# Strassen's gate and up products on normalised inputs, with one Silu operation and six steps' first products at the front

## The chip, the cores and the metric

The kernel runs on 1 core of one Trainium2 chip. The metric is device time in microseconds, the median of several executions. Besides them one execution is recorded by the hardware profiler. Engines are named as in the profile: PE (TensorE: matmuls), DVE (VectorE), ACT (ScalarE), POOL (GpSimd) and SP (which issues DMAs). Each engine works through its own instructions in order.

## The reference, cut to what matters

One layer of an encoder on 2048 new frames and 32 sample frames, width 1024. All matrices are float32. The change touches only the feed-forward part of the last frames:

```python
x = x + jnp.concatenate([att, pool], axis=-1) @ w_out
h2 = _rmsnorm(x, g_ffn)          # x * rsqrt(mean(x*x) + 1e-6) * g_ffn, per frame
x = x + (jax.nn.silu(h2 @ w_ffn_gate) * (h2 @ w_ffn_up)) @ w_ffn_down
gate = jax.nn.sigmoid(_rmsnorm(x, g_ple) @ w_ple_gate)
x = x + (p @ w_ple) * gate
```

`w_ffn_gate` and `w_ffn_up` are 1024 x 2816, `w_ffn_down` 2816 x 1024.

## The kernel before, in words

Activations lie with channels on partitions and frames in columns. Float32 accuracy comes from three matmuls per term (`mm3`, lines 214 to 216): each operand is split into a rounded high half and a low half, and high x high, high x low and low x high are summed in PSUM. A split (lines 179 and 180, for whole weight columns 198 and 199) is a cast on ACT and a subtraction on DVE.

The stage `rest` takes output blocks in three pairs; the last pair (b0 and b1, 352 frames each) is the `tail`. There the order is: output projection `w_out` with the residual, eight products per block (each 24 matmuls), then the feed-forward part, then the gated embedding. PE's order is the written order; the order of the other engines is a scheduler's.

In the tail the gate and up products use Strassen's scheme (Winograd's form): two halves of the 1024 input channels by two neighbouring output columns f and f+1 by two blocks b0 and b1, with seven products of quarter size (12 matmuls each) instead of eight. There are 22 steps, gate and up in turn. The products of a step, with weight x input, are: a11 x (b0, first half), a12 x (b0, second half), s1 x t1, s2 x t2, then s4 x (b1, second half), s3 x t3, a22 x t4. s1 to s4 are sums of the quarter weights, made by POOL (`sums`, line 960). t1 to t4 are sums over blocks and halves of the inputs (`combine`, made beside the projection of b1). The first product's result is copied out of PSUM by ACT as p1, the third (p5) stays in its bank until after the sixth, and the results are DVE additions (lines 1197, 1220, 1224, 1228).

The inputs before are x times the gain, without the per-frame factor of the norm (`rbc`, 1 / rms in every row). It is put in behind the products: `evac` multiplies a gate result by rbc (line 1179, DVE), takes Sigmoid (1181, ACT), multiplies by the result (1182, POOL) and by rbc once more (1187, POOL) for the up product; an up result is multiplied by that (1190, DVE) and split. `norm1` and `norm2` make rbc: column sums on PE, a power on POOL, a spread over partitions on PE, a copy by ACT. Down products of a group of output columns (`down`) stand behind the first step of the next group, those of the last group behind the last step.

Weights go through three buffers each of raw, high and low tiles (`RAW_BUFS, W_BUFS`); in the tail two units are prepared ahead of the one in use. PSUM banks of products rotate: `mm_bank` counts up, and in the tail six banks follow each other, so a product takes the bank of the product six before it:

```python
if phase["tail"] and phase["mm"] % 6 > 3:
    p, tag = ((ps_z, "z"), (ps_av, "av"))[phase["mm"] % 2]
    return p.tile([128, 512], F32, tag=tag, name=nm("mm"))
if phase["tail"] and phase["mm"] % 6 == 3 or ...
    return ps_x.tile([128, 512], F32, tag="x", name=nm("mm"))
return ps_mm.tile([128, 512], F32, tag="mm", name=nm("mm"))   # three banks
```

Of the kernel before, what the change touches and what calls it, by code (L numbers as in the profile page):

```python
# [78 lines left out]
def stickbreak_step(  # L79
# [794 lines left out]
    def rest(sup, pool, apool):  # L874
# [66 lines left out]
        def load_quad(wsrc, f):  # L941
# [5 lines left out]
            r = {"a11": a1[:, :4], "a12": a1[:, 4:]}  # L947
# [14 lines left out]
        QUADS = ("a11", "a12", "s1", "s2", "s4", "s3", "a22")  # L962
# [3 lines left out]
        def plan_quads():  # L966
            run = []

            def emit(items):
                hi = wpool.tile([128, 2, 4, 128], F32R, tag="whi", name=nm("whi"), bufs=W_BUFS)  # L970
                lo = wpool.tile([128, 2, 4, 128], F32R, tag="wlo", name=nm("wlo"), bufs=W_BUFS)
                for i, (j, key) in enumerate(items):
                    for n in (j, j + 1):
                        if n < len(steps) and n not in raws and (n == j or key == "s4"):
                            raws[n] = load_quad(*steps[n])
                    if key not in raws[j]:
                        sums(raws[j])
                    split(raws[j][key], hi[:, i], lo[:, i])
                return hi, lo, len(items)

            def close():
                for i in range(0, len(run), 2):
                    wplan.append(lambda items=run[i:i + 2]: emit(items))
                run.clear()

            for i, fs in enumerate(groups):
                FIRST[len(steps)] = i
                for f in fs[::2]:
                    steps.append((w_gate, f))
                    steps.append((w_up, f))  # L990
            for j in range(len(steps)):
                run.extend((j, key) for key in QUADS)
                i = FIRST.get(j)
                if i:
                    close()
                    plan_down(groups[i - 1])
            close()
            plan_down(groups[-1])

        quad = {"at": 0, "n": 0}  # L1000

        def next_quad():

            if quad["at"] == quad["n"]:
                quad["w"] = wunit()
                quad["at"], quad["n"] = 0, quad["w"][2]
            i = quad["at"]
            quad["at"] += 1
            return quad["w"][0][:, i], quad["w"][1][:, i]
# [23 lines left out]
        def combine(oc):  # L1033

            b0, b1 = sup
            k = oc % 4
            if oc < 4:
                H["d"] = tmp(b1, "t1")
                V.tensor_sub(H["d"], X[b1][oc], X[b0][oc])
                S.activation(H["d"], H["d"], AF.Copy, scale=gcol("ffn", oc))  # L1040
                keep_h("t1", k, H["d"])
                square(b1, oc)
                return
            def less(x, y):
                t = tmp(b1, "sg")
                V.scalar_tensor_tensor(out=t, in0=x, scalar=gcol("ffn", oc), in1=y, op0=ALU.mult, op1=ALU.subtract)
                return t
            ready_h(b1, oc, "ffn")
            t2 = less(X[b1][oc], H["d"])
            keep_h("t2", k, t2)  # L1050
            h12 = tmp(b1, "t2")
            S.activation(h12, X[b1][k], AF.Copy, scale=gcol("ffn", k))
            t3 = less(X[b1][oc], h12)
            t4 = tmp(b1, "t2")
            V.scalar_tensor_tensor(out=t4, in0=X[b0][oc], scalar=gcol("ffn", oc), in1=t2, op0=ALU.mult, op1=ALU.subtract)
            keep_h("t3", k, t3)
            keep_h("t4", k, t4)
# [4 lines left out]

        OC = {b: range(KC) for b in sup}
        if sup == OS[-1]:
            OC[sup[1]] = [c + 4 * e for c in range(4) for e in range(2)]
        for b in sup:
            for oc in OC[b]:
# [24 lines left out]
        for b in sup:  # L1092
            if b == 0:
                yield BUBBLE
            for i, oc in enumerate(OC[b]):
# [5 lines left out]
                if tail and b == sup[1]:  # L1101
                    combine(oc)
                    if i == 1:
                        norm1(sup[0])
                    if i == 3:
                        norm2(sup[0])
# [58 lines left out]
        def strassen():  # L1165
# [8 lines left out]
            def evac(j, x, b, t):  # L1174
# [3 lines left out]
                if src is w_gate:  # L1178
                    V.tensor_mul(t, t, rbc[b])  # L1179
                    sg = tmp(b, "sg")  # L1180
                    S.activation(sg, t, AF.Sigmoid)
                    GP.tensor_mul(sg, sg, t)
                    if x == 0 and b == b0:
                        g = ap.tile([128, 385], F32, tag="keep", name=nm("g"), bufs=5)[:, :n]
                    else:
                        g = pool.tile([128, OMAX], F32, tag="xs", name=nm("g"), bufs=X_SLOTS)[:, :n]
                    GP.tensor_mul(g, sg, rbc[b])
                    sgr[f, b] = g
# [10 lines left out]

            for j in range(len(steps)):  # L1200
                pa = mm_bank()[:, :n]
                yield from prod(pa, [h[b0][k] for k in range(4)])
                p1 = ap.tile([128, WMAX], F32, tag="bot", name=nm("p1"), bufs=3)[:, :n]
                S.copy(p1, pa)
# [259 lines left out]
```

## Time and profile before

| | |
|---|---|
| median of 3 runs | 2895.23 us (2890.81 to 2901.4) |
| profiled execution, its own time | 2899.64 us |
| its span, first to last instruction | 2897.9 us, mean granted clock 0.988 |
| PE, DVE, ACT, POOL busy | 97%, 76%, 47%, 28% |
| output projection of b1 ends, first step starts | about 2281 us |
| last step of the scheme ends | about 2761 us |

Times in the trace are microseconds from the span's start. A row of the timeline gives start, duration, engine, line, operation, tiles written and read, shape, and in square brackets the idle time before it and what ended it. PEclk is the granted clock of PE as a share of 2.4 GHz: 0.50 is the level of 1.2 GHz.

### The profile page before, as it was taken

The page shows a single profiled execution, that of the slowest core. Times are in us where ns is not written, and L with a number is a line of the kernel's source. Part 1 is how long each engine was busy: PE and PEld are TensorE (multiplying, and loading weights), DVE is VectorE, ACT ScalarE, POOL GpSimd, SP SyncE. Part 2 cuts the span into 40 slices and gives each one's busy share as a digit, 9 for nine tenths or more (in the row PEclk, how much of TensorE's full clock was granted, in tenths as well). Part 3 has the DMA queues.
Part 4 walks back from the last instruction along what each step waited for, and adds up shares of the span by engine and source line. Part 5 has one row for each costly group of instructions (what it writes and reads, how often), then busy time and mean ns, then how long its engine had stood idle before and what let it go on. Part 6 is the DMA issues. An engine that isn't in the chain of part 4 may idle for free. (4 is left out here: it accounts for less than half of the span.)

```text
span 2897.9 us, 50355 instructions
## 1 busy us (share of the span) xinstructions
PE 2796.9 (97%) x18214; PEld 2747.3 (95%) x18214; DVE 2202.5 (76%) x3738; ACT 1362.8 (47%) x2986; POOL 817.3 (28%) x1311
## 2 busy tenths in 40 slices
PE   8999999899999999989999999999999899999998
PEld 7998989899999999989999999999999899999998
DVE  6476798797877777887888777777555887787676
ACT  5455666464444444455554444444343532333343
POOL 2021233132222213232332211212132653554320
PEclk9999999899999999999999999999999999999999
DMA  6867747773333333323753243333236322221233
GB/s 206 240 191 209 217 147 226 227 221 94 106 103 100 94 93 94 110 86 110 223 143 97 88 123 103 96 103 98 86 88 202 114 70 73 73 74 58 63 90 119
DMA packets 522274, 366.51 MB, mean 126 GB/s; under 512 B 63005, under 2 KB 509277, under 8 KB 522026
## 3 DMA queue, kind: packets, MB, share of 16 engines
q1 hardware_dynamic: 483914, 350.51, 40.4%
q10 hardware_dynamic: 38112, 12.79, 1.7%
q8 instruction: 144, 2.36, 0.3%
q14 instruction: 104, 0.85, 0.1%
HBM read 292.89 MB, written 70.32 MB: 125 GB/s over the span
## 5 line engine op out<-in xcount | busy, mean ns | idle before, releaser
L214 PE MATMUL mm<-as,whi 128*128 128x352 f32 (+1 forms) x3628 | 1207.0, 333 | 27.4 <-DVE t L1197 19.6
L215 PE MATMUL mm<-as,whi 128*128 128x352 f32 (+1 forms) x3628 | 1170.4, 323 | 0.0
L216 PE MATMUL mm<-as,wlo 128*128 128x352 f32 (+1 forms) x3628 | 1165.8, 321 | 1.7 <-DVE wlo L180 1.1
L214 PEld LDWEIGHTS mm<-as,whi 128*128 128x128 f32 x3628 | 687.5, 190 | 34.0 <-issue 21.4
L216 PEld LDWEIGHTS mm<-as,wlo 128*128 128x128 f32 x3628 | 687.1, 189 | 2.5 <-DVE wlo L180 1.5
L215 PEld LDWEIGHTS mm<-as,whi 128*128 128x128 f32 x3628 | 686.9, 189 | 0.6 <-DVE as L913 0.3
L198 ACT CAST whi<-wraw 128x1024 fp32r<-128x1024 f32 x282 | 295.9, 1050 | 264.8 <-PE mm L215 248.5
L742 DVE TENSOR_TENSOR_SCAN keep<-keep,keep,zeros 128x384 f32<-128x384 f32 (+2 forms) x328 | 317.3, 967 | 112.4 <-ACT keep L727 111.6
L199 DVE TENSOR_TENSOR wlo<-wraw,whi 128x1024 fp32r<-128x1024 f32 x279 | 347.9, 1247 | 59.0 <-ACT whi L198 57.4
L727 ACT ACTIVATE keep<-z 128x384 f32<-128x384 f32 (+3 forms) x464 | 195.4, 421 | 361.7 <-PE z L724 305.7
L739 POOL COPY keep<-keep 128x1 f32<-128x1 f32 (+1 forms) x328 | 147.8, 451 | 442.2 <-DVE keep L742 441.7
L743 DVE TENSOR_TENSOR beta<-beta,keep 128x384 f32<-128x384 f32 (+3 forms) x464 | 237.8, 513 | 32.5 <-POOL beta L732 1.4
L180 DVE TENSOR_TENSOR aa<-tp,aa 128x384 fp32r<-128x384 f32 (+4 forms) x472 | 213.5, 452 | 14.4 <-ACT aa L179 13.2
L724 PE MATMUL z<-kt,q 128*128 128x384 f32 (+4 forms) x928 | 212.1, 310 | 12.5 <-ACT beta L728 12.3
L179 ACT CAST aa<-tp 128x384 fp32r<-128x384 f32 (+4 forms) x472 | 192.9, 409 | 62.3 <-PE tp L753 52.3
L1161 DVE TENSOR_TENSOR xs<-xs,mm 128x352 f32<-128x352 f32 (+1 forms) x288 | 143.6, 510 | 81.3 <-PE mm L216 80.0
L753 PE MATMUL tp<-ident,beta 128*128 128x128 f32 (+1 forms) x1112 | 199.7, 274 | 2.2 <-DVE xt L342 1.5
L214 PE MATMUL mm<-hh,whi 128*128 128x384 f32 (+2 forms) x576 | 198.9, 345 | 2.3 <-ACT yt L457 1.0
L906 POOL TENSOR_TENSOR acc<-acc,sq 128x352 f32<-128x352 f32 (+1 forms) x112 | 119.7, 1068 | 285.3 <-ACT sq L905 277.1
L728 ACT ACTIVATE beta<-z 128x384 f32<-128x384 f32 (+3 forms) x464 | 194.4, 419 | 7.2 <-ACT keep L727 5.2
L1140 POOL TENSOR_TENSOR sg<-sg,t 128x336 f32<-128x336 f32 (+1 forms) x88 | 103.1, 1171 | 324.5 <-ACT sg L1115 313.6
L215 PE MATMUL mm<-hl,whi 128*128 128x384 f32 (+2 forms) x576 | 186.5, 324 | 1.2 <-DVE hl L336 1.2
(202 smaller groups left out, 4660.2 us busy)
## 6 DMA issues: line engine op xcount, KB each, us to landing
wraw<-in_w_ffn_down_dram SPq DMA_DIRECT2D x66, 512.0 KB, 3.5
wraw<-in_w_ffn_gate_dram SPq DMA_DIRECT2D x55, 512.0 KB, 3.9
wraw<-in_w_ffn_up_dram SPq DMA_DIRECT2D x55, 512.0 KB, 4.0
wraw<-in_w_in_dram SPq DMA_DIRECT2D x48, 512.0 KB, 4.9
wraw<-in_w_out_dram SPq DMA_DIRECT2D x48, 512.0 KB, 5.3
kt<-ks SPq DMA_DIRECT2D x112, 192.0 KB, 2.5
vt<-vs SPq DMA_DIRECT2D x112, 192.0 KB, 2.8
wraw<-in_w_ple_gate_dram SPq DMA_DIRECT2D x32, 512.0 KB, 4.0
```

Of the source, the lines that this page charges most:

```text
L180: V.tensor_sub(lo, src, hi.bitcast(F32))
L198: S.copy(hi, raw)
L199: eng.tensor_sub(lo, raw, hi.bitcast(F32))
L214: T.matmul(ps, a[0], b[0], start=first, stop=False)
L215: T.matmul(ps, a[0], b[1], start=False, stop=False)
L216: T.matmul(ps, a[1], b[0], start=False, stop=last)
L724: T.matmul(z[:qw, :wi], hd["q"][:, e, qsl], un["k"][:, :wi], start=(e == 0), stop=(e == 1))
L727: S.activation(keep[:qw, :wi], z[:qw, :wi], AF.Sigmoid, scale=-0.125)
L728: S.activation(beta[:qw, :wi], z[:qw, :wi], AF.Sigmoid, scale=0.125)
L742: V.tensor_tensor_scan(rev, rev, zeros[:qw].broadcast_to([qw, wi]), initial=init, op0=ALU.mult, op1=ALU.add)
L743: V.tensor_mul(beta[:qw, :wi], beta[:qw, :wi], keep[:qw, 1:wi + 1])
L753: T.transpose(bank[:kw, qo[i]:qo[i] + qws[i]], un["b"][i][:qws[i], k0:k0 + kw], ident[:qws[i], :qws[i]])
```

## The change

The inputs of the scheme are normalised (gain and rbc in one DVE operation, `normed`), so a gate result needs one ACT operation, Silu, and an up result is multiplied by it. b0's inputs are made beside b1's projection (`first_inputs`); b1's and t1 to t4 need b1's norm and are made after it (`other_inputs`). Two products of a step, those that read b0 alone, become a helper `front`; those of the first six steps (`AHEAD`) run ahead of everything else, and b1's norm and `other_inputs` are written behind the first and second of them. Units of weights no longer run over steps: a11 with a12 (one split of a whole column), s1 with s2, s4 with s3, a22 alone. The first column of the first six steps is loaded once more for the front.

```diff
-        QUADS = ("a11", "a12", "s1", "s2", "s4", "s3", "a22")
+        UNITS = (("a11", "a12"), ("s1", "s2"), ("s4", "s3"), ("a22",))
+        AHEAD = 6
...
+            for j in range(AHEAD):
+                plan_col(steps[j][0], steps[j][1] * 128)
             for j in range(len(steps)):
-                run.extend((j, key) for key in QUADS)
...
+                for keys in UNITS[j < AHEAD:]:
+                    wplan.append(lambda j=j, keys=keys: emit(j, keys))
...
-        def combine(oc):
...
+        def normed(t, b, c):
+            V.scalar_tensor_tensor(out=t, in0=X[b][c], scalar=gcol("ffn", c), in1=rbc[b], op0=ALU.mult, op1=ALU.mult)
+            return t
+        def first_inputs(c):
...
+            H["n", c] = normed(H["pair"][:, c % 2, :N[sup[0]]], sup[0], c)
+            keep_h("h11" if c < 4 else "h21", c % 4, H["n", c])
+        def other_inputs():
...
+            for k in range(4):
+                h12[k] = normed(tmp(b1, ("acc", "sg")[k // 2]), b1, k)
+                t1 = tmp(b1, "t1")
+                V.tensor_sub(t1, h12[k], H["n", k])
+                keep_h("t1", k, t1)
+            for k in range(4):
+                h22 = normed(extra(), b1, 4 + k)
+                t3 = tmp(b1, "t2")
+                V.tensor_sub(t3, h22, h12[k])
+                t2 = extra()
+                V.tensor_add(t2, t3, H["n", k])
+                keep_h("t2", k, t2)
+                keep_h("h22", k, h22)
+                keep_h("t3", k, t3)
+                t4 = tmp(b1, "t1")
+                GP.tensor_sub(t4, H["n", 4 + k], t2)
+                keep_h("t4", k, t4)
...
                 if src is w_gate:
-                    V.tensor_mul(t, t, rbc[b])
-                    sg = tmp(b, "sg")
-                    S.activation(sg, t, AF.Sigmoid)
-                    GP.tensor_mul(sg, sg, t)
...
-                    GP.tensor_mul(g, sg, rbc[b])
...
+                    S.activation(g, t, AF.Silu)
...
+            def front(j):
+                pa = mm_bank()[:, :n]
+                yield from prod(pa, [H["h11", k] for k in range(4)])
...
+                S.copy(p1[j], pa)
+                pa = mm_bank()[:, :n]
+                yield from prod(pa, [H["h21", k] for k in range(4)])
+                evac(j, 0, b0, plus("t1", pa, p1[j]))
+            for j in range(AHEAD):
+                yield from front(j)
+                if j == 0:
+                    norm1(b1)
+                if j == 1:
+                    norm2(b1)
+                    other_inputs()
             for j in range(len(steps)):
...
+                if j >= AHEAD:
+                    yield from front(j)
```

DVE at the front. Before, the end of the last combination (t2, t3, t4 of the eighth channel block) stands right ahead of the first step's first addition (L1197):

```order
L913 SCALAR_TENSOR_TENSOR as_6030_28915<-xs_6028_28887,gt_95,as_6030_28915 128x352
L1046 SCALAR_TENSOR_TENSOR sg_6032_28921<-xs_6028_28887,gt_95,t1_6018_28863 128x352
L1046 SCALAR_TENSOR_TENSOR sg_6035_28928<-xs_6028_28887,gt_95,t2_6034_28926 128x352
L1055 SCALAR_TENSOR_TENSOR t2_6036_28930<-xs_5927_28453,gt_95,sg_6032_28921 128x352
L180 TENSOR_TENSOR as_6033_28923<-sg_6032_28921,as_6033_28923 128x352
L180 TENSOR_TENSOR t3_6008_28816<-sg_6035_28928,t3_6008_28816 128x352
L180 TENSOR_TENSOR t4_6038_28935<-t2_6036_28930,t4_6037_28934 128x352
L180 TENSOR_TENSOR wlo_6041_28940<-s3_6026_28879,whi_6040_28939 128x512
L1197 TENSOR_TENSOR t1_6047_28978<-mm_6046_28965,p1_6045_28963 128x352
```

Now the end of `other_inputs` stands ahead of the third front pair's addition (L1198, t1_6069, which reads mm_6068), and the fourth pair's stands four rows on:

```order
L1031 SCALAR_TENSOR_TENSOR hx_6055_29014<-xs_5988_28794,gt_95,rbc_6010_28913 128x352
L180 TENSOR_TENSOR as_6049_28999<-hx_6048_28997,as_6049_28999 128x352
L180 TENSOR_TENSOR as_6050_29002<-hx_6046_28993,as_6050_29002 128x352
L180 TENSOR_TENSOR t4_6054_29011<-t1_6052_29008,t4_6053_29010 128x352
L1057 TENSOR_TENSOR t2_6056_29016<-hx_6055_29014,sg_6024_28943 128x352
L1059 TENSOR_TENSOR hx_6057_29018<-t2_6056_29016,hn_5958_28650 128x352
L180 TENSOR_TENSOR t3_6051_29005<-t2_6056_29016,t3_6051_29005 128x352
L1198 TENSOR_TENSOR t1_6069_29068<-mm_6068_29055,p1_6067_29053 128x352
L180 TENSOR_TENSOR as_6058_29020<-hx_6057_29018,as_6058_29020 128x352
L180 TENSOR_TENSOR as_6059_29023<-hx_6055_29014,as_6059_29023 128x352
L180 TENSOR_TENSOR t4_6062_29031<-t1_6060_29028,t4_6061_29030 128x352
L1198 TENSOR_TENSOR t1_6077_29106<-mm_6076_29093,p1_6075_29091 128x352
```

What moved: all additions of the front from the third pair on are queued behind the 42 rows of `other_inputs` and the weight splits among them.

DVE in a gate step (step 8). Before, an rbc multiply (L1179) follows each of the four results:

```order
L1197 TENSOR_TENSOR t1_6360_30658<-mm_6357_30639,p1_6356_30637 128x352
L1179 TENSOR_TENSOR t1_6360_30658<-t1_6360_30658,rbc_5985_28715 128x352
L180 TENSOR_TENSOR wlo_6366_30681<-wraw_6351_30599,whi_6365_30680 128x512 x2
L1197 TENSOR_TENSOR t2_6367_30698<-mm_6364_30679,p1_6356_30637 128x352
L1197 TENSOR_TENSOR acc_6368_30700<-mm_6363_30666,t2_6367_30698 128x352
L1220 TENSOR_TENSOR acc_6368_30700<-mm_6369_30702,acc_6368_30700 128x352
L180 TENSOR_TENSOR wlo_6374_30724<-s1_6375_30725,whi_6373_30723 128x512
L1179 TENSOR_TENSOR acc_6368_30700<-acc_6368_30700,rbc_6059_29032 128x352
L180 TENSOR_TENSOR wlo_6374_30724<-s2_6376_30727,whi_6373_30723 128x512
L1224 TENSOR_TENSOR t2_6367_30698<-mm_6372_30722,t2_6367_30698 128x352
L1197 TENSOR_TENSOR t1_6379_30750<-mm_6363_30666,t2_6367_30698 128x352
L1179 TENSOR_TENSOR t1_6379_30750<-t1_6379_30750,rbc_6059_29032 128x352
```

Now the step holds additions and weight splits alone:

```order
L1198 TENSOR_TENSOR t1_6364_30608<-mm_6363_30595,p1_6362_30593 128x352
L180 TENSOR_TENSOR wlo_6368_30614<-a22_6328_30419,whi_6367_30613 128x512
L1198 TENSOR_TENSOR t2_6370_30642<-mm_6369_30629,p1_6362_30593 128x352
L1198 TENSOR_TENSOR acc_6371_30644<-mm_6366_30612,t2_6370_30642 128x352
L180 TENSOR_TENSOR wlo_6374_30648<-wraw_6357_30569,whi_6373_30647 128x1024
L1236 TENSOR_TENSOR acc_6371_30644<-mm_6372_30646,acc_6371_30644 128x352
L1240 TENSOR_TENSOR t2_6370_30642<-mm_6376_30666,t2_6370_30642 128x352
L180 TENSOR_TENSOR wlo_6381_30686<-s1_6382_30687,whi_6380_30685 128x512
L1198 TENSOR_TENSOR t1_6377_30680<-mm_6366_30612,t2_6370_30642 128x352
L180 TENSOR_TENSOR wlo_6381_30686<-s2_6383_30689,whi_6380_30685 128x512
L1244 TENSOR_TENSOR t2_6370_30642<-mm_6379_30684,t2_6370_30642 128x352
```

What moved: four rows are gone, and the whole first column of the next step is split in one row.

POOL after b1's norm (r_6001), now: the sums of steps 0 and 1 (L960) and the four subtractions that make t4 (L1064, into t1 tiles):

```order
L268 TENSOR_TENSOR r_6001_28871<-ss_5999_28863,mhalf_93 128x3
L252 MEMSET ss_7149_34742 128x3
L960 TENSOR_TENSOR s2_6086_29123<-s1_6085_29121,wraw_6080_29113 128x512
L960 TENSOR_TENSOR s3_6087_29125<-wraw_6080_29113,a21_6081_29115 128x512
L960 TENSOR_TENSOR s4_6088_29127<-wraw_6080_29113,s2_6086_29123 128x512
L960 TENSOR_TENSOR s1_6112_29247<-a21_6095_29167,a22_6096_29169 128x512
L1064 TENSOR_TENSOR t1_6034_28966<-hn_5967_28696,hx_6030_28955 128x352
L960 TENSOR_TENSOR s3_6114_29251<-wraw_6094_29165,a21_6095_29167 128x512
L960 TENSOR_TENSOR s2_6113_29249<-s1_6112_29247,wraw_6094_29165 128x512
L1064 TENSOR_TENSOR t1_6043_28987<-hn_5967_28696,hx_6039_28976 128x352
L960 TENSOR_TENSOR s4_6115_29253<-wraw_6094_29165,s2_6113_29249 128x512
L1064 TENSOR_TENSOR t1_6052_29008<-hn_5976_28742,hx_6048_28997 128x352
```

What moved: the t4 subtractions, DVE's before, stand in POOL's queue among the weight sums.

## Rows read from the trace of the kernel before

**Rows 1.** The page: busy time, share and instructions of each engine.

```profile
PE 2796.9 (97%) x18214; PEld 2747.3 (95%) x18214; DVE 2202.5 (76%) x3738; ACT 1362.8 (47%) x2986; POOL 817.3 (28%) x1311
```

**Rows 2.** PE's waits, 2180 to 2898 us: total, times, longest.

```profile
PE mm L214 <- DVE t L1197: 19.6, 10, 5.4
PE mm L214 <- ACT as L179: 4.5, 1, 4.5
```

**Rows 3.** Busy time by stretches: length, PE, PEld, DVE, ACT, POOL, PEclk, DMA.

```profile
2275.00:2330.00 55.00, 46.32 (x264) 44.73 (x263) 47.80 (x72) 24.35 (x49) 33.93 (x27) 0.91 0.26 76
2330.00:2690.00 360.00, 340.15 (x2070) 336.51 (x2069) 282.24 (x410) 116.33 (x212) 176.70 (x133) 0.98 0.24 72
2690.00:2770.00 80.00, 74.79 (x451) 73.70 (x450) 56.09 (x86) 23.82 (x43) 23.54 (x19) 0.96 0.20 60
2510.00:2570.00 60.00, 60.00 (x376) 59.82 (x375) 42.59 (x64) 17.64 (x34) 26.79 (x20) 1.00 0.23 67
...
2582.00:2586.00 4.00, 4.00 (x14) 4.00 (x15) 3.88 (x6) 2.27 (x5) 2.07 (x2) 0.50 0.00 0
```

**Rows 4.** DVE's timeline from a gate step's end into the up step.

```profile
2386.02 1.26 DVE L1179 TENSOR_TENSOR t<-t,rbc 128x352 f32<-128x352 f32 x1
2387.21 1.77 DVE L180 TENSOR_TENSOR wlo<-s,whi 128x512 fp32r<-128x512 f32 x1
...
2399.99 0.52 DVE L1197 TENSOR_TENSOR t<-mm,t 128x352 f32<-128x352 f32 x1
```

**Rows 5.** PE's timeline, the two places named.

```profile
2400.66 0.41 PE L214 MATMUL mm<-as,whi 128*128 128x352 f32 x1 [3.45 <-DVE t L1197]
...
2766.06 0.66 PE L214 MATMUL mm<-as,whi 128*128 128x352 f32 x1 [4.53 <-ACT as L179]
```

**Rows 6.** DVE's timeline while POOL stands still.

```profile
2281.38 0.57 DVE L1055 SCALAR_TENSOR_TENSOR t<-xs,gt,sg 128x352 f32<-128x352 f32 x1
2281.88 0.52 DVE L180 TENSOR_TENSOR as<-sg,as 128x352 fp32r<-128x352 f32 x1
2282.31 0.52 DVE L180 TENSOR_TENSOR t<-sg,t 128x352 fp32r<-128x352 f32 x1
...
2283.18 0.68 DVE L180 TENSOR_TENSOR wlo<-wraw,whi 128x512 fp32r<-128x512 f32 x1
...
2284.82 0.52 DVE L1039 TENSOR_TENSOR t<-xs,xs 128x352 f32<-128x352 f32 x1
```

**Rows 7.** DVE's timeline while POOL works without a break.

```profile
2269.68 2.31 DVE L199 TENSOR_TENSOR wlo<-wraw,whi 128x1024 fp32r<-128x1024 f32 x1
2271.92 0.51 DVE L1100 TENSOR_TENSOR xs<-xs,mm 128x352 f32<-128x352 f32 x1
...
2274.15 1.60 DVE L1039 TENSOR_TENSOR t<-xs,xs 128x352 f32<-128x352 f32 x1
```

**Rows 8.** POOL's timeline in the same stretch.

```profile
2269.44 1.48 POOL L960 TENSOR_TENSOR s<-s,wraw 128x512 f32<-128x512 f32 x1 [1.37 <-DMA wraw<-in_w_ffn_gate_dram]
2270.88 2.27 POOL L960 TENSOR_TENSOR s<-wraw,a 128x512 f32<-128x512 f32 x1
2273.10 2.27 POOL L960 TENSOR_TENSOR s<-wraw,s 128x512 f32<-128x512 f32 x1
```

**Rows 9.** Groups by line and form, 2240 to 2766 us: count, busy, mean.

```profile
L180 DVE TENSOR_TENSOR wlo<-s,whi 128x512 fp32r<-128x512 f32 x88 | 80.9, 929 | 0.7 <-ACT whi L179 0.2
L1187 POOL TENSOR_TENSOR g<-sg,rbc 128x352 f32<-128x352 f32 x44 | 55.1, 1255 | 2.1
L1179 DVE TENSOR_TENSOR t<-t,rbc 128x352 f32<-128x352 f32 x33 | 31.0, 940 | 0.8
```

**Rows 10.** DVE's timeline ahead of the last product group.

```profile
2761.39 1.23 DVE L199 TENSOR_TENSOR wlo<-wraw,whi 128x1024 fp32r<-128x1024 f32 x1
2762.53 0.52 DVE L1190 TENSOR_TENSOR t<-t,g 128x352 f32<-128x352 f32 x1
```

**Rows 11.** Groups by line: the activation table load.

```profile
L727 ACT ACT_TABLE_LOAD x1 | 1.3, 1283 | 0.0
```

More of the change, by code (lines that the diff above doesn't have):

```diff
@@ L946, in load_quad @@
             dma(a1, w[:, :, :128])
[L947 removed]
+            r = {"a1": a1, "a11": a1[:, :4], "a12": a1[:, 4:]}
             for key, k in (("a21", 0), ("a22", 4)):
@@ L966, in plan_quads, with emit @@
         def plan_quads():
[L967 to L976, printed above, removed]
-                        sums(raws[j])
[L978 to L984, printed above, removed]
+            def emit(j, keys):
+                for n in (j, j + 1):
+                    if n < len(steps) and n not in raws and (n == j or keys[0] == "s4"):
+                        raws[n] = load_quad(*steps[n])
+                hi = wpool.tile([128, KC, 128], F32R, tag="whi", name=nm("whi"), bufs=W_BUFS)
+                lo = wpool.tile([128, KC, 128], F32R, tag="wlo", name=nm("wlo"), bufs=W_BUFS)
+                if keys[0] == "a11":
+                    split(raws[j]["a1"], hi, lo)
+                else:
+                    if keys[0] == "s1":
+                        sums(raws[j])
+                    for i, key in enumerate(keys):
+                        split(raws[j][key], hi[:, 4 * i:4 * i + 4], lo[:, 4 * i:4 * i + 4])
+                return hi, lo, len(keys)
             for i, fs in enumerate(groups):
@@ new lines, in first_inputs, with extra @@
+        def first_inputs(c):
+            if c % 2 == 0:
+                H["pair"] = apool.tile([128, 2, OMAX], F32, tag="as", name=nm("hn"), bufs=ACT_SLOTS)
+            H["n", c] = normed(H["pair"][:, c % 2, :N[sup[0]]], sup[0], c)
+            keep_h("h11" if c < 4 else "h21", c % 4, H["n", c])
+        def other_inputs():
+            b1 = sup[1]
+            def extra():
+                return pool.tile([128, OMAX], F32, tag="xs", name=nm("hx"), bufs=X_SLOTS)[:, :N[b1]]
+            h12 = {}
+            for k in range(4):
[15 more added lines that the diff above has]
+                keep_h("t4", k, t4)
@@ L1059, in h_terms @@
         def h_terms(w, b):
             return [(kpart(w, k), h[b][k]) for k in range(KC)]
-        OC = {b: range(KC) for b in sup}
-        if sup == OS[-1]:
-            OC[sup[1]] = [c + 4 * e for c in range(4) for e in range(2)]
         for b in sup:
-            for oc in OC[b]:
+            for oc in range(KC):
                 plan_col(w_out, oc * 128)
@@ L1094, in rest @@
                 yield BUBBLE
-            for i, oc in enumerate(OC[b]):
+            for i, oc in enumerate(range(KC)):
                 wu = wunit()
@@ L1100, in rest @@
                 V.tensor_add(X[b][oc], X[b][oc], ps)
[L1101 to L1106, printed above, removed]
+                if tail:
+                    square(b, oc)
+                    if b == sup[1]:
+                        if i == 0:
+                            norm1(sup[0])
+                        if i == 1:
+                            norm2(sup[0])
+                        if 2 <= i < 6:
+                            first_inputs(2 * i - 4)
+                            first_inputs(2 * i - 3)
                 else:
```

65 lines of the change are left out of this document (16 added, 49 removed).

## The prediction, made blind

> **What bounds the kernel now.** The page comes first: TensorE (PE) is busy 97% of a 2897.9 us span [rows 1]. Where PE is full, time can come only from its gaps and from slow clock, so the next view is PE's own waits from 2180 us on, the last pair of output blocks, which is all that the change touches: 19.6 us in ten waits for VectorE (DVE) line L1197, and 4.5 us once for a split of the last product [rows 2]. The reader is to see that PE waits there for DVE, never for a transfer.
>
> The table by stretches gives the loss with clock included. From 2510 to 2570 us PE has no gap at clock 1.00 and issues 376 matmuls in 60 us, so 0.160 us each [rows 3]; a product of 12 takes 1.92 us. By that rate, 2275 to 2330 (the front: end of the output projection, steps 0 and 1) does 264 x 0.160 = 42.1 us of work in 55, a loss of **12.9**; 2330 to 2690 does 330.3 in 360, a loss of **29.7**; 2690 to 2770 does 72.0 in 80, a loss of **8.0** [rows 3]. Together 50.6 us. Part of it is clock: after a gap the granted clock is 0.50, the 1.2 GHz level, for 2582 to 2586 us: 14 matmuls where 25 fit, 1.8 us [rows 3]. I count 2 us behind each long gap.
>
> What makes DVE late is read in its timeline around one gap. PE's second product of a step waits until 2400.66 us for a PSUM bank that L1197 frees at 2400.5 [rows 4, 5]; banks rotate over six products, and this is the one that holds p5. That addition could follow p5's last use, the t3 product, at once; two products (3.84 us) and a wait of 3.45 lie between, so it is some 7 us behind, 6 of them lateness. Ahead of it stand a multiply by rbc of 1.26 us and a weight split of 1.77 us [rows 4]. Alone, these forms take 0.52 and 0.68; an operation starts some 0.08 before the one ahead has ended, so they count 0.43 and 0.60, a normalisation 0.50 [rows 6]. They are long while GpSimd (POOL) works: with POOL running three operations back to back from 2269.44 [rows 8], a whole weight split takes 2.31 instead of 1.23 [rows 7, 10] and a subtraction 1.60 instead of 0.52 [rows 7, 6], some 1.1 us more each, while an addition that reads PSUM stays at 0.51 [rows 7]. So POOL's work is DVE's delay.
>
> **The change part by part.** *Gate.* Gone are 44 DVE multiplies by rbc (33 of them are in [rows 9], 940 ns each) and 88 POOL multiplies (44 of them 1255 ns each [rows 9]); one Silu stands for one Sigmoid. Silu has no row. By the nearest ones, ScalarE (ACT) operations of the same 352 columns, it is some 0.5 us; ACT is busy 47% [rows 1], so twice that hides too. Two table loads of 1.3 us [rows 11] come in, both on ACT: cost 0, at most 2.6.
>
> Ledger of one gate step and the up step behind it, for DVE, in starts: before, 14 half splits x 0.60, 14 additions, 4 rbc multiplies and 8 operations of the up step x 0.43 = 19.5 us; the 16 POOL operations in it at 0.9 add 14.4: 33.9 us, where PE needs 14 x 1.92 = 26.9. That is why PE waits. After: 17.8, and 8 POOL operations (weight sums) add 7.2: 25.0, under 26.9. What would be late next, the splits of s1 and s2, has 1.9 us to spare per pair.
>
> In the first three pairs the change takes two products out of each step: PE 19.2, DVE 13.8 + 7.2 = 21.0, 1.8 late per pair. The down product behind step 2 takes up part of the 5.4: I take 4 us, with 2 for all later pairs. So the middle's 29.7 becomes **6**. Bounds: 2 (POOL's delay much smaller) and 15 (half of the loss comes from splits queued ahead, not from the gate).
>
> *Front.* Before, the combinations t1 to t4 were made during the projection, and the loss was 12.9. Now only block b0's inputs are made there (8 normalisations, 8 splits, per projection product some 3.4 us of DVE and 1 POOL operation against PE's 3.84: hidden). Then six steps' pairs of first products run, 12 products, 23.0 us of PE; b1's norm comes behind the first and second pair, and all of `other_inputs` only then. Let E be the end of the projection. PE ends the second pair at E + 7.7. DVE then has an addition, a multiply, a whole split (1.14) and a split: 2.4 us, so the inputs start at E + 10.1. From there to the addition that follows them stand 42 rows in DVE's order: 8 normalisations x 0.50, 12 additions x 0.44, 17 splits x 0.43, one whole weight split 1.14 and four half ones x 0.60 [rows 6, 10] = 20.1 us. POOL runs about ten operations in that time (four sums of step 1, most of step 0's, three of the t4 subtractions). At 0.9 each, 9 us more: E + 39.2, and the addition for the third pair ends at E + 39.6. It frees the bank that the twelfth front product needs; PE gets there at E + 11 x 1.92 = E + 21.1. So PE idles **18.5 us** once, with 2 of slow clock: 20.5 instead of 12.9. (The small norm matmuls delay both sides alike and are left out.)
>
> The price of one POOL operation decides here. The row shows 1.1 us where DVE had nothing but SBUF work [rows 7, 8]; over the whole stage the half split's mean is 929 ns, 0.25 over its 0.68 [rows 9, 6]. I take 0.9, nearest to the crowded row, as the queue is crowded. Bounds: no delay, 9.5 idle + 2 = 11.5; the whole length of a POOL operation, 1.48 [rows 8], and 4 us of ACT, POOL and DVE handing t4 round, 28.3 + 2 = 30.
>
> The rows show the form with two SBUF inputs stopped and the PSUM one not [rows 7, 8]. The Trainium skill, SBUF — State Buffer, "Who interferes with whom", says the same: VectorE operations with two SBUF inputs and GpSimd share a port pair that is locked for a whole instruction, and the second one blocks fully. By that rule ten operations cost some 14.8 us and not 9, the front 26.3, and the kernel 2884, inside the likeliest case's own range below; by the row, 2878. The trace is between full and partial, as DVE's extra 1.1 is shorter than the POOL operation beside it.
>
> *End.* The last gap, 4.53 us [rows 5], has two whole weight splits queued ahead of the last multiply [rows 10]; their places don't change. The 8.0 becomes **7** (5 to 8).
>
> *Weights.* Each step takes its seven quarter matrices in four units (three pairs and a single one) instead of three and a half, in the same three buffers. The lead is then at times three products, 5.8 us, instead of four. Six first columns are loaded twice; PE waited for no transfer [rows 2].
>
> **The sum.** 20.5 - 12.9 + 6 - 29.7 + 7 - 8.0 = -17.1 us. The profiled execution took 2899.64 us, 4.4 over the median of 2895.23; the difference is applied to the median: **2878 us**. With the likeliest case's bounds (front 16 to 25, middle 4 to 9) it is 2870 to 2887. All lower bounds give 11.5 + 2 + 5 = 18.5 of loss instead of 50.6, 2863; all upper ones 30 + 15 + 8 = 53, 2898.
>
> **Rivals.** *Inputs hidden, chance 0.20.* POOL hardly delays DVE in the front; for it: the mean of 929 ns. Loss 11.5 + 3 + 6 = 20.5, time 2865.
>
> *The bank wait eats the gain, 0.17.* The front at 30 and the middle at 13, as half the lateness stays: 30 + 13 + 7 = 50, time 2895. For it: DVE, POOL and ACT are in-order, and t4 passes through all three four times. Against it: DVE's queue after the change has less than PE's in the full steps.
>
> *Weights come late, slower, 0.13.* Place: the start of each of the 22 steps, where the third matmul waits for a low half whose unit had a lead of 5.8 us. DVE was up to 6 us late in an up step [rows 4, 5], and with a single matrix in each step that lateness would now exceed the lead. Price: 6 us, and 1.2 for the split itself [rows 10], less 5.8 is 1.4, with a share of slow clock 1.8; times 22 steps 40 us in place of the 6: 20.5 + 40 + 7 = 67.5, time 2912. It decides from 1.1 us a step, where the middle passes 23 us. Against it: the rows that show lateness are those under gate work that goes away.
>
> That the change doesn't do what it says (ACT reloading tables at every Silu) is excluded by ACT's order, which has two loads in addition.
>
> **How the numbers follow.** Forecast 0.50. A difference under 0.3% (8.7 us) can't be told from none here: 2886.5 to 2904 counts as the same. The forecast and the hidden case are faster: 0.70. The eaten gain is the same: 0.17. Late weights: 0.13, slower. The range of 2863 to 2898 leaves out the slower case and little else.
>
> **What would show it.** One PE wait of 10 to 25 us some 21 us behind the end of the projection, released by the DVE addition of the new helper; no L1197-type wait over 1 us in the full steps; DVE's half splits near 0.8 us in the mean; POOL busy some 110 us less (88 operations of 1.25); a clock of 0.50 right behind the long wait. The prediction is wrong if PE waits at low halves of weights, if the long wait is under 8 us, or if the waits in the up steps stay.

## The result and the profile after

The changed kernel takes **2880.48 us** (median of 6 runs, 2879.1 to 2883.71), the kernel before 2895.34 (6 runs beside it). The ratio is 0.9949, with a 95% interval of 0.9936 to 0.9962: 0.5% faster. The forecast was 2878. The profiled executions, 2899.64 and 2879.16 us, lie 20.5 apart, the medians 14.9; the forecast difference of 17.1 lies between.

The page's busy times, for [rows 1]:

```profile
PE 2787.4 (97%) x18214; PEld 2742.6 (95%) x18214; DVE 2158.4 (75%) x3684; ACT 1360.4 (47%) x2958; POOL 718.7 (25%) x1227
```

POOL has lost 98.6 us and DVE 44.1, PE has the same matmuls. PE's waits from 2180 us on (total, times, longest), for [rows 2]:

```profile
PE mm L214 <- DVE t L1198: 19.8, 2, 17.3
PE mm L214 <- ACT as L179: 2.6, 1, 2.6
PE mm L216 <- DVE wlo L199: 1.7, 1, 1.7
```

Ten waits for an addition have become two, one of 17.3 us. Busy time by stretches (length, then PE, PEld, DVE, ACT, POOL with their instructions, PEclk, DMA), for [rows 3]; the projection ends at about 2278.5 us now:

```profile
2320.00:2324.00 4.00, 4.00 (x14) 4.00 (x15) 3.41 (x8) 2.95 (x7) 0.21 (x1) 0.50 0.00 0
2270.00:2325.00 55.00, 36.06 (x215) 35.48 (x214) 45.65 (x69) 26.01 (x49) 23.47 (x17) 0.84 0.33 96
2325.00:2385.00 60.00, 59.99 (x374) 59.70 (x374) 48.55 (x76) 18.75 (x35) 22.71 (x16) 1.00 0.30 88
2385.00:2665.00 280.00, 277.45 (x1721) 277.19 (x1720) 204.63 (x297) 97.30 (x165) 81.37 (x56) 0.99 0.25 74
2665.00:2745.00 80.00, 77.39 (x482) 77.04 (x480) 52.28 (x83) 26.35 (x43) 11.94 (x8) 1.00 0.24 71
```

At 60 us per 376 matmuls the losses are 20.7 in the front, 0.3 and 5.4 in the middle, 3.1 at the end: 29.5 where 50.6 were lost before. Right behind the long wait the granted clock is 0.50, with 14 matmuls in 4 us, as in the row of before. PE's gaps themselves, for [rows 5]:

```profile
2300.79 0.43 PE L216 MATMUL mm<-as,wlo 128*128 128x352 f32 x1 [1.69 <-DVE wlo L199]
2319.91 0.66 PE L214 MATMUL mm<-as,whi 128*128 128x352 f32 x1 [17.25 <-DVE t L1198]
...
2392.43 0.40 PE L214 MATMUL mm<-as,whi 128*128 128x352 f32 x1 [2.55 <-DVE t L1198]
...
2744.66 0.66 PE L214 MATMUL mm<-as,whi 128*128 128x352 f32 x1 [2.62 <-ACT as L179]
```

DVE in the front: the second pair's addition, the first row of `other_inputs`, one row that waits for t4 to come round by ACT, and the third pair's addition that ends the long wait:

```profile
2286.70 0.53 DVE L1198 TENSOR_TENSOR t<-mm,p 128x352 f32<-128x352 f32 x1 [2.39 <-PE mm L216]
...
2290.39 3.13 DVE L1031 SCALAR_TENSOR_TENSOR acc<-xs,gt,rbc 128x352 f32<-128x352 f32 x2
...
2305.35 1.06 DVE L180 TENSOR_TENSOR t<-t,t 128x352 fp32r<-128x352 f32 x1 [1.33 <-ACT t L179]
...
2319.34 0.52 DVE L1198 TENSOR_TENSOR t<-mm,p 128x352 f32<-128x352 f32 x1
```

From 2290.39 to 2319.34 are 28.95 us for the rows that take 20.1 alone. Beside them POOL has ten operations, six sums and four t4 subtractions. The groups by line and form, 2240 to 2745 us, for [rows 9], with Silu's duration (column: count, busy, mean, idle before):

```profile
L180 DVE TENSOR_TENSOR wlo<-s,whi 128x512 fp32r<-128x512 f32 x88 | 92.7, 1067 | 1.8 <-ACT whi L179 1.3
...
L960 POOL TENSOR_TENSOR s<-wraw,a 128x512 f32<-128x512 f32 x22 | 33.1, 1506 | 133.2 <-DVE wlo L180 133.2
...
L1189 ACT ACTIVATE g<-t 128x352 f32<-128x352 f32 x33 | 16.4, 498 | 28.0 <-DVE t L1198 24.6 <-DVE t L1244 3.4
```

Silu costs the half microsecond taken for it. But the half weight splits are longer than before (929 ns), although POOL works 98.6 us less: its sums wait for a split to free their buffer (133.2 us of idle time before one of the four) and then run beside the next split, which they stop (below).

### The profile page after: what moved, and what is told of

Same layout as the page of the kernel before. It is cut to its first block, busy times and chain, and to the rows that moved or that the text cites. A ratio compares the mean times of both kernels' runs of the same rounds, so it can differ in the third digit from the quotient of the medians.

```text
span 2877.4 us, 50102 instructions
## 1 busy us (share of the span) xinstructions
PE 2787.4 (97%) x18214; PEld 2742.6 (95%) x18214; DVE 2158.4 (75%) x3684; ACT 1360.4 (47%) x2958; POOL 718.7 (25%) x1227
## 4 chain that ended last, share of the span: by engine, by line
PE 75%; DVE 12%; issue 5%; ACT 3%; DMA 3%; POOL 1%; SPq 0%; ACTq 0%; DVEq 0%; POOLq 0%
PE mm L214 21%; PE mm L215 21%; PE mm L216 21%; PE z L724 4%; PE tp L753 3%; DVE keep L742 2%; PE av L766 2%; PE av L767 2%; DVE wlo L199 2%; DVE as L913 1%; DVE beta L743 1%; DVE win L429 1%; DVE aa L180 1%; ACT whi L198 1%; ACT as L912 1%
## 5 line engine op out<-in xcount | busy, mean ns | idle before, releaser
L198 ACT CAST whi<-wraw 128x1024 fp32r<-128x1024 f32 x288 | 302.4, 1050 | 274.7 <-PE mm L215 262.1
L199 DVE TENSOR_TENSOR wlo<-wraw,whi 128x1024 fp32r<-128x1024 f32 x285 | 349.3, 1225 | 58.3 <-ACT whi L198 56.9
L180 DVE TENSOR_TENSOR aa<-tp,aa 128x384 fp32r<-128x384 f32 (+4 forms) x472 | 213.4, 452 | 13.8 <-ACT aa L179 12.6
L216 PE MATMUL mm<-hh,wlo 128*128 128x384 f32 (+2 forms) x576 | 185.9, 323 | 0.4 <-DVE wlo L199 0.4
```

Source lines behind the costliest of these rows:

```text
L180: V.tensor_sub(lo, src, hi.bitcast(F32))
L198: S.copy(hi, raw)
L199: eng.tensor_sub(lo, raw, hi.bitcast(F32))
L216: T.matmul(ps, a[1], b[0], start=False, stop=last)
```

## Experiments

All are edits of the changed kernel except `b_units`, an edit of the kernel before. Ratios are to the kernel before on the same chip; the changed kernel has 0.9949 [0.9936, 0.9962].

| kernel | median us | ratio [95%] |
|---|---|---|
| e_pool: two POOL multiplies beside the gate | 2880.27 | 0.9939 [0.9922, 0.9956] |
| e_dve: one DVE multiply beside the gate | 2882.47 | 0.9946 [0.9927, 0.9964] |
| e_actpath: one DVE multiply ahead of Silu | 2882.96 | 0.9952 [0.9937, 0.9967] |
| e_poolpath: two POOL multiplies behind Silu | 2883.27 | 0.9956 [0.9941, 0.9971] |
| e_beside: all three, beside the gate | 2897.94 | 1.0003 [0.9992, 1.0014] |
| e_chain: the whole old chain | 2900.72 | 1.0011 [1.0002, 1.0021] |
| e_units: the old packing of weights | 2879.62 | 0.9939 [0.9924, 0.9954] |
| b_units: before, with units closed at each step | 2896.39 | 1.0000 [0.9991, 1.0009] |
| e_nosums: no sums in steps 0 and 1 | 2879.06 | 0.9940 [0.9923, 0.9956] |
| e_pieces: inputs in five pieces | 2876.58 | 0.9929 [0.9914, 0.9944] |
| e_early_t4: pieces, earlier norm, t4 on DVE | 2873.78 | 0.9924 [0.9908, 0.9941] |
| e_two: two pairs ahead instead of six | 2877.31 | 0.9938 [0.9922, 0.9955] |

**What gave the middle's gain: POOL's work or DVE's?**

`e_pool`, behind Silu in `evac`:

```diff
+                    if x or b == b1 or j >= AHEAD:
+                        z = tmp(b, "sg")
+                        GP.tensor_mul(z, g, rbc[b])
+                        GP.tensor_mul(z, z, rbc[b])
```

> The changed kernel with two POOL multiplications put back for each gate result outside the front (41 of 44 results, 82 operations into a scratch tile that nobody reads, each some 1.25 us as before the change). PE's and DVE's own instructions are those of the changed kernel. Theory A, POOL's work was what made DVE late: DVE's ledger for a full pair goes from 25.0 to 17.8 + 16 x 0.9 = 32.2 us against PE's 26.9, so waits of several us come back in the up steps, the stretch behind the front loses 15 us more or beyond, and the median is 2893 to 2905. Rival B, DVE's own rbc multiplications were it: at most 5 us more, 2880 to 2886. Rival C, the gain came from the order of weight units alone: no difference, 2878 to 2884.

`e_dve`, in the same place:

```diff
+                        z = tmp(b, "sg")
+                        V.tensor_mul(z, g, rbc[b])
```

> The changed kernel with one DVE multiplication by rbc put back for each gate result outside the front (41 of 44, into a scratch tile); POOL stays as in the changed kernel. Theory A (POOL's work made DVE late): DVE's ledger for a full pair goes from 25.0 to 26.7 us against PE's 26.9, so 0 to 6 us more, median 2880 to 2887. Rival B (DVE's own multiplications were it): most of the middle's loss comes back, 12 us or more, 2893 to 2900. Rival C (order of weight units): no difference.

Neither slowed the kernel clearly: both intervals overlap the changed kernel's. So theory A, the prediction's own reason, fell in this form, and B alone too. What was left: the chain's place on the path, the order of the weight units (C), or both kinds of work together.

**The chain on the path, and the packing.** `e_chain` replaces the Silu line:

```diff
-                    S.activation(g, t, AF.Silu)
+                    V.tensor_mul(t, t, rbc[b])
+                    sg = tmp(b, "sg")
+                    S.activation(sg, t, AF.Sigmoid)
+                    GP.tensor_mul(sg, sg, t)
+                    GP.tensor_mul(g, sg, rbc[b])
```

> The changed kernel with the old gate chain put back on every gate result outside the front: DVE multiplies the sum by rbc, ACT takes Sigmoid, POOL multiplies twice (41 DVE and 82 POOL operations, and the result comes later); the gate's values are then not those of the reference. The two halves alone (POOL's two multiplies beside the path, DVE's one beside the path) cost nothing and 2 to 3 us. Theory A2 (the chain counts because it stands on the path: the up product's multiply and ACT's casts queue behind it): PE's waits for an addition in the middle (2328 to 2669) come back to 15 to 25 us from 2.5, and the median is 2892 to 2900. Rival C (the middle's gain came from the order of the weight units): waits under 8 us, median 2881 to 2886, the sum of what the halves cost.

`e_units` packs all blocks of a group in one run again:

```diff
-                for keys in UNITS[j < AHEAD:]:
-                    wplan.append(lambda j=j, keys=keys: emit(j, keys))
+                run.extend((j, key) for keys in UNITS[j < AHEAD:] for key in keys)
...
+                    close()
```

> The changed kernel with the weights packed as before: the blocks of all the steps of a group in one run, two at a time, so that a unit can hold blocks of two steps, and the first two blocks of a step are split as two halves; Silu, the normalised inputs and the six-fold front stay. Theory A2 (the gate chain made the middle's waits): waits for an addition in the middle under 6 us, median 2879 to 2883. Rival C (the packing made them, by splits that wait for a buffer ahead of an addition that PE waits for): such waits 12 to 25 us, median 2888 to 2900.

`b_units`:

```diff
                 run.extend((j, key) for key in QUADS)
+                close()
                 i = FIRST.get(j)
```

> The kernel before with the units closed at the end of each step (no unit holds blocks of two steps, four units a step instead of three and a half); the old gate chain, the old inputs and the short front stay. Theory A2: the middle's waits stay at 15 to 25 us, median 2892 to 2898. Rival C: they fall under 6 us and the median is 2870 to 2882.

C fell twice. In `b_units` PE's waits show how: those for an addition went down to 0.2 us, and others took their place, 17.4 us in eight, while the time stayed:

```profile
PE mm L214 <- ACT whi L179: 17.4, 8, 3.5
...
PE mm L214 <- DVE t L1196: 0.2, 1, 0.2
```

The packing decides which wait is seen, not how much is lost. The chain brought the kernel's time back to that of before: A2's time, but its waits for additions came to only 6.4 us (23.6 less the long one of 17.2), beside 5.5 for low halves and others. It did not bring back all of the middle's loss. The front of `e_chain` is still the changed kernel's, which loses 7.8 us more than the old one (20.7 against 12.9). From the projection's end to the last product group it takes 487.5 us, the changed kernel 466.2 and the kernel before some 485; so behind the front some 21 of the 27 us that the change gains there came back. What the other 6 are isn't shown: old packing and old chain together on the new front weren't tried. Was it the path?

**Path or sum.** `e_actpath` puts the DVE multiply ahead of Silu, `e_poolpath` the two POOL multiplies between Silu and g, `e_beside` the same three operations where nothing waits for them:

```diff
 e_actpath
+                        V.tensor_mul(t, t, rbc[b])
                     S.activation(g, t, AF.Silu)
 e_poolpath
+                    S.activation(sg, t, AF.Silu)
+                    GP.tensor_mul(sg, sg, t)
+                    GP.tensor_mul(g, sg, rbc[b])
 e_beside
                     S.activation(g, t, AF.Silu)
+                        z = tmp(b, "sg")
+                        GP.tensor_mul(z, g, rbc[b])
+                        GP.tensor_mul(z, z, rbc[b])
+                        V.tensor_mul(tmp(b, "zd", 1), g, rbc[b])
```

> The changed kernel with one DVE multiply by rbc put ahead of Silu for every gate result outside the front (41), so that ACT's operation, and the casts behind it in ACT's order, wait for it; no POOL operation; the gate's values are then not those of the reference. The whole old chain on the path gave 2900.7, its parts beside the path 2880.3 and 2882.5. Theory H1 (ACT waits in order for DVE's multiply, and its casts come late for DVE's splits): ACT's idle time before the gate operation is about 80 us in the middle as with the whole chain (45 in the changed kernel), median 2891 to 2899. Theory H3 (no single path, the work of both engines together): median 2881 to 2885.

> The changed kernel with POOL's two multiplies put between Silu and the gate value for every gate result outside the front (82), so that POOL holds the addition's buffer and the gate value comes some 2.5 to 4 us later; no DVE operation; the gate's values are then not those of the reference. Theory H2 (what counts is that the buffer and the value come free late): median 2891 to 2899, waits of the up product's multiply or of additions for POOL. Theory H1 or H3: median 2880 to 2884, no wait for POOL over 1 us.

> The changed kernel with the same work as the old chain, one DVE and two POOL multiplies for every gate result outside the front, all beside the path: nothing waits for their results but their own buffers. Theory H3 (the work of both engines together fills DVE's time): median 2892 to 2900. Theories H1 and H2 (the place in the chain): the sum of the two alone, median 2881 to 2885.

The sum decides (H3). On the path or beside it, DVE's multiplies alone or POOL's alone move the median by 3 us at most; both together cost some 16 to 17, although nothing waits for their results. The same cycle of work (two gate and two up steps and a down product group, from the first output row of one `down` to that of the next) in one line each, first the changed kernel:

```profile
2502.78:2587.40 84.62, 84.62 (x530) 84.62 (x529) 60.49 (x89) 28.62 (x48) 23.40 (x16) 1.00 0.26 76
```

`e_pool`:

```profile
2503.89:2588.49 84.60, 84.60 (x530) 84.60 (x529) 62.13 (x90) 28.45 (x48) 44.83 (x33) 1.00 0.26 75
```

`e_dve`:

```profile
2512.91:2598.29 85.38, 85.22 (x532) 84.93 (x531) 64.69 (x97) 28.05 (x48) 22.97 (x16) 1.00 0.25 77
```

`e_beside`:

```profile
2520.19:2606.90 86.71, 83.84 (x520) 82.96 (x518) 70.03 (x98) 27.51 (x49) 44.29 (x33) 1.00 0.24 74
```

`e_chain`:

```profile
2523.26:2610.85 87.59, 85.05 (x527) 84.08 (x527) 68.71 (x97) 27.92 (x48) 44.93 (x33) 1.00 0.25 73
```

The kernel before:

```profile
2510.68:2599.59 88.91, 83.52 (x507) 83.07 (x507) 68.86 (x101) 28.53 (x52) 43.25 (x33) 0.96 0.24 72
```

Read the third busy time, DVE's, against the length. PE's own work is 28 products of 12 and 192 matmuls of `down`, 528 x 60/376 = 84.3 us (a row's x can miss a few). At 60 and 62 us of DVE the cycle is PE's; at 65 it is 0.8 us longer, but PE is idle for only 0.2 of that, which is no clear sign; at 69 to 70 it is 2 to 4 us longer, and PE idles. The place of the limit shows when the rows of the down group (its splits L199 and its additions to `xs`) are left out: the other rows of DVE take 48, 49 and 52 us in the first three kernels and 57, 56 and 56 in the last three, and the 28 products of the four steps beside which most of them run take PE 28 x 1.92 = 53.8. The 17 POOL multiplies alone add 1.6 us to DVE, 0.1 each; the 8 DVE multiplies alone 4.2, 0.5 each; together they add 9.5, not 5.8. The extra DVE multiply shows why, in the groups of `e_dve`, 2512 to 2599 us:

```profile
L1192 DVE TENSOR_TENSOR sg<-g,rbc 128x352 f32<-128x352 f32 x9 | 5.8, 649 | 1.1 <-ACT g L1189 1.1
```

and of `e_beside`, 2520 to 2607 us:

```profile
L1194 DVE TENSOR_TENSOR zd<-g,rbc 128x352 f32<-128x352 f32 x9 | 10.1, 1119 | 1.1 <-ACT g L1189 1.1
```

The same operation takes 649 ns, and 1119 where POOL multiplies the same gate value. From the projection's end to the last product group 7 of the 41 such rows are stretched in `e_dve`, all by weight sums, and 25 of 41 in `e_beside`, 24 of them by POOL's multiplies, which wait for the same Silu. POOL's 82 multiplies stop 31 rows of DVE in `e_pool`, for 11.4 us in all, and 57 in `e_beside`, for 30.8.

**The front: what the long wait is made of.** `e_nosums` leaves the eight weight sums out:

```diff
-                    if keys[0] == "s1":
+                    if keys[0] == "s1" and j > 1:
                         sums(raws[j])
+                    elif keys[0] == "s1":
+                        raws[j].update(s1=raws[j]["a21"], s2=raws[j]["a22"], s3=raws[j]["a21"], s4=raws[j]["a22"])
```

> The changed kernel without the eight weight sums of steps 0 and 1 (the unsummed quarters are used in their place, so this part of the product is left out); all else the same. In the front POOL then runs only the four t4 subtractions instead of ten to eleven operations beside the 42 rows. Theory A (each POOL operation costs DVE 0.9 us there): the long PE wait falls from 17.3 + 1.7 us by 6 or 7 x 0.9, to 12 to 14 us, and the median by some 5 to 8 us, to 2873 to 2876. With the whole length of a POOL operation as price (1.5) it falls to 8 to 10 us. Rival D, POOL's work is hidden and the 42 rows alone are the length: the wait stays at 18 to 19.

PE's gaps in it, and POOL's first sum of step 2:

```profile
2312.93 0.66 PE L214 MATMUL mm<-as,whi 128*128 128x352 f32 x1 [12.33 <-DVE t L1200]
...
2343.99 0.63 PE L214 MATMUL mm<-as,whi 128*128 128x352 f32 x1 [5.03 <-DVE t L1200]
```

```profile
2332.54 1.29 POOL L960 TENSOR_TENSOR s<-a,a 128x512 f32<-128x512 f32 x1 [19.31 <-DMA a<-in_w_ffn_gate_dram]
```

The front's idle time fell from 18.9 to 12.3 us, by 6.6. Seven of the eight sums ran there (the other one before the projection's end): 0.94 us each, theory A's price. DVE's 42 rows went from 28.95 to 23.2 us; their start and the addition behind them in `e_nosums`:

```profile
2289.16 1.07 DVE L1033 SCALAR_TENSOR_TENSOR acc<-xs,gt,rbc 128x352 f32<-128x352 f32 x2
...
2312.36 0.52 DVE L1200 TENSOR_TENSOR t<-mm,p 128x352 f32<-128x352 f32 x1
```

The first two rows take 1.07 us without sums and 3.13 with them. Six sums ran beside the 42 rows, so a sum costs 0.96 there; what is left over the 20.1 us of rows and the wait for ACT, 1.75 us, is the four t4 subtractions, 0.44 each. Why 0.96 of a sum of some 1.5 us, is read in the changed kernel by putting single DVE rows beside POOL's:

```profile
2288.84 1.62 DVE L180 TENSOR_TENSOR as<-t,as 128x352 fp32r<-128x352 f32 x1
2294.81 1.62 DVE L180 TENSOR_TENSOR t<-t,t 128x352 fp32r<-128x352 f32 x1
2307.80 1.58 DVE L1031 SCALAR_TENSOR_TENSOR hx<-xs,gt,rbc 128x352 f32<-128x352 f32 x1
```

```profile
2288.39 1.70 POOL L960 TENSOR_TENSOR s<-s,wraw 128x512 f32<-128x512 f32 x1 [4.39 <-DMA wraw<-in_w_ffn_gate_dram]
2294.49 1.55 POOL L960 TENSOR_TENSOR s<-a,a 128x512 f32<-128x512 f32 x1 [1.36 <-DMA a<-in_w_ffn_up_dram]
2307.61 1.39 POOL L960 TENSOR_TENSOR s<-s,wraw 128x512 f32<-128x512 f32 x1 [1.59 <-DVE wlo L180]
```

Alone the three DVE rows take 0.52, 0.52 and 0.58 us. Each ends as if it had started only 0.13 to 0.2 us before POOL's operation ended (2290.46 - 0.52 = 2289.94, against 2290.09). So a row is stopped until POOL's operation ends, and it loses what is then left of that operation, not its whole length. From the projection's end to the last product group 68 rows of the changed kernel, and 111 of the kernel before, are over 0.15 us longer than alone; the same holds for every one of them, and none loses more than 1.13 us.

The time did not follow: 5 us came back at once, because step 2's weights landed at 2332.5 (2328.0 in the changed kernel), its four sums ran late and DVE's splits of them stood ahead of the addition that PE waited for.

`e_pieces` hands out `other_inputs` over five pairs, by a `yield` at the end of its second loop:

```diff
                 if j == 1:
                     norm2(b1)
-                    other_inputs()
+                    inputs = other_inputs()
+                if j >= 1:
+                    next(inputs, None)
```

> The changed kernel with other_inputs written in five pieces, one behind each front pair from the second on, so that the additions that free the banks stand between the pieces in DVE's queue. Theory A, the front waits for the sum of DVE's queue: the single wait of 17.3 us for the third pair's addition goes, but PE then waits as long in sum for later additions and for the inputs of the second combination; the sum of PE's idle time in the front is 15 to 19 us and the median within 4 us of the changed kernel's, 2877 to 2884. Rival E, it is the bank alone that holds PE, as one addition stands too late: most of the wait goes, the idle sum is under 8 us and the median 2866 to 2871.

Its waits in the front, 2284 to 2330 us:

```profile
PE mm L214 <- ACT as L179: 10.9, 4, 4.2
PE mm L215 <- DVE as L180: 3.7, 3, 2.0
```

The 14.6 us and 2876.58 are just under A's 15 and 2877, and far over E's 8 and 2871: a free bank alone doesn't free PE, which next waits for DVE's queue itself. `e_early_t4` adds two edits:

```diff
-                GP.tensor_sub(t4, H["n", 4 + k], t2)
+                V.tensor_sub(t4, H["n", 4 + k], t2)
...
-                yield from front(j)
+                yield from front(j, (lambda: norm2(b1)) if j == 1 else None)
```

`front` calls that function behind its `S.copy`, so the broadcast of b1's norm stands behind the first product of the second pair.

> The changed kernel with the second block's inputs made in five pieces behind the second to sixth front pair, the broadcast of its rsqrt put behind the first product of the second pair instead of behind its second, and the four t4 subtractions on DVE instead of POOL. The pieces alone gave 2876.6. Theory A (the front lasts as long as DVE's queue): DVE starts the inputs some 2 us earlier, and four operations at 0.82 us of delay become four at 0.52 us: the front's idle time falls from 14.6 to 11 to 13 us, median 2872.5 to 2875.5. Rival (the pairs wait for the hand-over of banks and sums, not for the amount of work): idle time 14 to 16 us, median 2876 to 2878.

The waits there are 12.6 us (11.5, 0.9 and 0.2), the median 2873.78, both as A had them; which of the two edits did it isn't separated. It is the fastest kernel here; its interval still overlaps the changed kernel's.

**What the six pairs ahead are worth.** `e_two`:

```diff
-        AHEAD = 6
+        AHEAD = 2
```

> The changed kernel with two steps' first products at the front instead of six; the inputs are normalised, Silu and the units stay, and b1's inputs are still made in one piece behind the second pair. Theory A (the front lasts as long as DVE's queue, and PE needs b1's inputs for everything behind the pairs done ahead): PE has two products' pairs and the five products of the first step to do until the last input is ready some 40 us after the projection's end, so its idle time there is 22 to 26 us against 18.9, less some 4 us for the four column splits that DVE no longer has: 19 to 23 in several waits, median 2880 to 2885. Rival F (the pairs ahead are what hides the inputs: eight products less at the front, 15.4 us more idle time): 30 to 35 us idle, median 2892 to 2897.

It took 2877.31 us: both expectations were too slow. DVE makes the inputs in one go, with no weight split among the rows and one weight sum beside them; the first row and the addition behind the last:

```profile
2291.19 1.07 DVE L1031 SCALAR_TENSOR_TENSOR acc<-xs,gt,rbc 128x352 f32<-128x352 f32 x2
...
2314.33 0.53 DVE L1198 TENSOR_TENSOR t<-mm,p 128x352 f32<-128x352 f32 x1 [0.18 <-PE mm L216]
```

That is 23.1 us where the changed kernel has 28.95, and the waits for the inputs sum to 12.4 us in small pieces, at a granted clock of 0.78 from 2273 to 2328 us (0.84 in the changed kernel). The six-fold front buys nothing that these runs can measure: the gain of the change is, as far as the runs tell, that of the normalised inputs and Silu.

## Why the prediction was right, and where not

- **What bounds the stage**: right. Nearly all that is lost is PE waiting for DVE, before and after, and the loss by stretches accounts for the time: 50.6 - 29.5 = 21.1, spans 20.5 apart.
- **Gate, the middle's 6**: 5.7 measured. The size was right and the reason half right. The gain does come from DVE's and POOL's multiplies together, which the change takes away so that DVE's need falls under PE's, as the ledger has it. The term that failed is "the 16 POOL operations in it at 0.9". With it, POOL's multiplies alone would have kept a pair at 25.0 + 8 x 0.9 = 32.2 us against PE's 26.9; `e_pool` has no loss. Alone a POOL multiply adds 0.1 us to DVE's busy time there, and with DVE's multiplies back 0.3 (70.03 - 64.69 over 17). The ledger put the old pair 7.0 us over PE; the cycle above shows 4.6 for two pairs and a down group, in which DVE has room. The price was too high, as it was taken for every POOL operation alike, whatever DVE has in hand when it runs. Once DVE's need is under PE's, only PE counts; that the middle still came out at 5.7 is in this part luck.
- **Half splits near 0.8 us**: wrong, 1067 ns, as sums released by one split stop the next. It cost no time that shows: PE is full in the changed kernel's cycle above.
- **POOL busy some 110 us less**: 98.6; four t4 subtractions (6.6 us) came in.
- **No wait over 1 us in full steps**: right. The one of 2.55 at 2392.43 stands in step 5, the last of the six whose first products ran ahead (its next addition reads p1 from `sq`, at 2396.05); for these the ledger had DVE 1.8 us late per pair.
- **Front, 18.5 idle and 2 of clock**: 17.25 and 1.69 of waits, and 20.7 with clock. The path was as worked out, with E = 2278.5: inputs from E + 11.9 (forecast 10.1), the third pair's addition done at E + 41.4 (39.6), PE at the bank at E + 24.2 (21.1). The price of 0.9 holds here for a sum (0.96), not for a t4 subtraction (0.44); over the ten operations it is (28.95 - 20.1 - 1.33) / 10 = 0.75. The prediction read the rows as a delay "between full and partial". That reading was wrong: a stopped row waits to the end of POOL's operation. By the Trainium skill's page SBUF — State Buffer, section "SBUF: two separate sides", when a VectorE operation with two SBUF inputs meets a GpSimd operation that reads SBUF, the one that starts first holds the ports they share for its whole instruction, and the other is blocked. The trace agrees, with the stopped rows above. The 14.8 us for ten operations priced each at its whole length; a row loses only what is left when it comes up, and where POOL came second, POOL waited (the t4 subtraction at 2301.75 took 3.04 us, with four DVE rows running at full speed beside it).
- **End, 7**: 3.1. The last gap fell from 4.53 to 2.62, which the prediction had excluded as the splits' places don't change. It stands at 2.6 in every kernel whose middle is full, and at 4.5 to 4.6 in `e_chain`, `e_beside` and `b_units`: that DVE comes to the end late from the steps fits this, and wasn't tried by itself.
- **Weights**: no late weights but one low half, 1.69 us in the front, which the sum had not priced. The slower rival did not come. Nor did the hidden inputs (9.5 us of idle time, against 18.9) or the eaten gain.

## What to carry to other kernels

Work beside the critical engine has a price only from a point on: here neither DVE's extra multiplies nor POOL's did anything clear alone, and together they cost the whole gain. So taking away either would have brought nearly all of it. Find the point by putting pieces back one by one, on and off the path. Where a queue has no room (the front), every sum of POOL's delays the end (0.96 us of some 1.5). There, making the work in pieces gave the two lowest medians (2876.6 and 2873.8), though their intervals overlap that of the changed kernel.

## What had not been expected of the hardware

What a POOL operation costs DVE depends on what DVE has in hand then. A row with two SBUF inputs that comes up meanwhile is stopped until POOL's operation ends; a row that reads PSUM is not (507 to 525 ns in the 108 rows that ran wholly beside a POOL operation, before and after). So a weight sum costs 0.96 us in the front, where DVE runs SBUF work back to back, and a multiply 0.1 us in a cycle of `e_pool`. The extra busy time of the two engines isn't additive: 1.6 and 4.2 us alone, 9.5 together in one cycle, as DVE's extra rows are those that POOL's extra operations stop.
